# Masked softmax: whole stores held for the load four batches on, and narrow loads as four one-packet transfers

## Chip, cores and metric

One core of a Trainium2 chip runs the whole kernel. The metric is the device time of one execution in microseconds (us); the time of a kernel is the median of its runs.

## What is computed

The reference is a softmax over the last axis of `x`, of shape 16 batches x 8 heads x 256 x 256 in float32. In batch `b` only the first `lengths[b]` columns take part; the others are zero in the result.

```python
for b in range(batch):
    length = lengths[b]
    masked = x[b, :, :, :length].copy()
    masked = masked - np.max(masked, axis=-1, keepdims=True)
    exp_masked = np.exp(masked)
    result[b, :, :, :length] = exp_masked / np.sum(exp_masked, axis=-1, keepdims=True)
```

The lengths of this input are, for batches 0 to 15: 188, 233, 229, 243, 195, 252, 165, 210, 222, 180, 209, 157, 159, 199, 214, 248.

## The kernel before

**Tiling.** A batch has 2048 rows of 256 numbers. They lie on 128 partitions with 16 rows each, so a batch is 16 KB per partition and 2 MB in all. The tile `xt` has 8 slots of one batch each; batch `b` lives in slot `b % 8`, and every step works in place.

**Loads.** Batches 0 to 3 are loaded whole by the SP queue (L107 to L111, batch 0 in two halves). Batches 4 to 15 are loaded by the POOL queue (L153 to L160). There the length is read into a register, and a ladder of branches (`pick`, L126) chooses the narrowest of the widths 160, 168, ... 240 that covers it, or the full 256. A narrow load moves only `w` columns of every row, that is rows of 4·w bytes: widths 200, full, 168, 216, 224, 184, 216, 160, 160, 200, 216, full for batches 4 to 15. Ten of the twelve are narrow. A load on POOL is one transfer. Load `n` waits for load `n - 2` (semaphore `s_sw`, L158) and for the store of batch `n - 8`, which frees its slot (`s_st`, L159). The first of them waits for batch 2 (L152).

**Work on a batch.** DVE masks the batch (L195; `clip` writes a very negative number over the columns past the length). ACT takes the exponential of each of the 16 row groups and sums it (L252), in two halves of eight. DVE then divides each half (L219 the reciprocal, L222 the product over 2048 elements). DVE runs one fixed order, L230 ff.: for batch 0 and from batch 4 on it is divide first half of `b`, mask `b + 1`, divide second half of `b`; for batches 1 to 3 the mask comes first.

**Stores.** The SP queue stores each batch in pieces (`parts`, L50): batch 0 whole, 1 to 7 as a half and two quarters, 8 to 12 and 15 as two halves, 13 and 14 whole. A piece waits for the half that it needs (L117), and the first piece of batch `b` for the whole store of batch `b - 2` (L119).

SP, POOL and ACT each have a queue of their own; all transfers run on the same 16 DMA engines.

Of the kernel before, what the change touches and what calls it, by code (L numbers as in the profile page):

```python
# [16 lines left out]
POOL = mybir.EngineType.Pool  # L17
# [3 lines left out]
def kernel(  # L21
# [6 lines left out]
    nc = tc.nc  # L28
    P = nc.NUM_PARTITIONS

    batch, heads, seq_q, seq_k = x.shape
    rows = heads * seq_q
    assert rows % P == 0
    nt = rows // P
    half = nt // 2
    quarter = nt // 4

    x_f = x.rearrange("b h q k -> b (h q) k").rearrange("b (p t) k -> b p t k", p=P)
    out_f = out.rearrange("b h q k -> b (h q) k").rearrange("b (p t) k -> b p t k", p=P)

    slots = 8
    ahead = 4
    assert slots - ahead == 4 and batch % slots == 0

    widths = list(range(160, 248, 8))
# [1 line left out]
    mid = seq_k // 2  # L47
    big = 1.0e30

    def parts(b):  # L50


        if b == 0:
            cuts = [0, nt]
        elif b < 8:
            cuts = [0, half, half + quarter, nt]
        elif b < 13 or b == batch - 1:
            cuts = [0, half, nt]
        else:
            cuts = [0, nt]  # L60
        return [slice(i, j) for i, j in zip(cuts, cuts[1:])]

    pool = ctx.enter_context(tc.tile_pool(name="all", bufs=1))
    psum = ctx.enter_context(tc.tile_pool(name="psum", bufs=1, space=bass.MemoryType.PSUM))
    xt = pool.tile([P, slots, nt, seq_k], F32, name="xt")
# [11 lines left out]
    seed = pool.tile([1, 2], F32, name="seed")  # L77

    sem = lambda n: ctx.enter_context(nc.semaphore(n))
    s_st = [sem("s_st0"), sem("s_st1")]  # L80
    with tc.tile_critical(no_gpsimd_drain=True):  # L81
# [3 lines left out]
        s_lenf = sem("s_lenf")  # L85
        s_ld = [sem(f"s_ld{k}") for k in range(ahead + 1)]

        s_sw = [sem("s_sw0"), sem("s_sw1")]

        s_iota = sem("s_iota")  # L90
        s_fill = sem("s_fill")
# [2 lines left out]
        s_exp = sem("s_exp")  # L94
        s_out = sem("s_out")

        def length(engine, at):

            return nc.values_load(  # L99
                at,  # L100
                engines=[engine],
                skip_runtime_bounds_check_because="compared with constants, never an address",
            )
# [3 lines left out]
        for h in range(2):  # L107
            s = slice(h * half, (h + 1) * half)
# [1 line left out]
        for b in range(1, ahead):  # L110
            nc.sync.dma_start(out=xt[:, b], in_=x_f[b]).then_inc(s_ld[b + 1], 16)  # L111

        nc.sync.wait_ge(s_exp, 3)
        for b in range(batch):
            s_b = s_st[b % 2]
            for s in parts(b):
                nc.sync.wait_ge(s_out, 2 * b + (s.stop - 1) // half + 1)  # L117
                if b >= 2 and s.start == 0:
                    nc.sync.wait_ge(s_b, 64 * (b // 2 + 1))  # L119
                nc.sync.dma_start(  # L120
                    out=out_f[b, :, s, :], in_=xt[:, b % slots, s, :]
                ).then_inc(s_b, 16 * ((s.stop - s.start) // quarter))

        def pick(v, n, slot, par, ws):  # L126

            if len(ws) == 1:
                w = ws[0]
                nc.gpsimd.dma_start(  # L130
                    out=xt[:, slot, :, :w], in_=x_n[:, n, :, :w]
                ).then_inc(s_sw[par], 16)
                return
            m = (len(ws) - 1) // 2
            with nc.gpsimd.If(v <= ws[m]):  # L135
                pick(v, n, slot, par, ws[: m + 1])
            with nc.gpsimd.Else():
                pick(v, n, slot, par, ws[m + 1 :])

        x_n = x_f.rearrange("b p t c -> p b t c")  # L140
        nc.gpsimd.iota(  # L141
# [1 line left out]
        ).then_inc(s_iota, 1)  # L143
        nc.gpsimd.memset(ones, 1.0).then_inc(s_ones, 1)  # L144
        for par in range(2):
            nc.gpsimd.memset(seed[:, par : par + 1], 0.0).then_inc(s_st[par], 64)  # L146
        nc.gpsimd.wait_ge(s_v, 2)
        for b in range(ahead, slots):
            nc.gpsimd.memset(xt[:, b, :, low:], 0.0).then_inc(s_fill, 1)  # L149
        nc.gpsimd.wait_ge(s_word, 16)  # L150
        nc.gpsimd.wait_ge(s_fill, slots - ahead)
        nc.gpsimd.wait_ge(s_ld[ahead - 1], 16)  # L152
        with nc.Fori(0, (batch - ahead) // 2, 1, engines=[POOL]) as q:  # L153
            for par in range(2):
                n = 2 * q + (ahead + par)
                v_len = length(POOL, word[0:1, bass.ds(2 * n, 1)])
                with nc.gpsimd.If(q >= 1):
                    nc.gpsimd.wait_ge(s_sw[par], 16 * q)  # L158
                    nc.gpsimd.wait_ge(s_st[par], 64 * q)  # L159
                pick(v_len, bass.ds(n, 1), bass.ds(n % slots, 1), par, widths + [seq_k])  # L160


        nc.tensor.wait_ge(s_ones, 1)
# [4 lines left out]
        v = 0  # L168

        def step(ins):  # L170
# [8 lines left out]
                out=down, in0=iota_i, scalar1=0.5, scalar2=-big, op0=ALU.add, op1=ALU.mult  # L179
# [7 lines left out]
                out=len_s, in0=len_f, scalar1=big, scalar2=None, op0=ALU.mult  # L187
# [4 lines left out]
        def clip(b, s, lo, hi):  # L192

            t = xt[:, b % slots, s, lo:hi]
            return nc.vector.scalar_tensor_tensor(  # L195
                out=t,
                in0=down[:, None, lo:hi].to_broadcast([P, s.stop - s.start, hi - lo]),
                scalar=len_s[:, b : b + 1],
                in1=t,
                op0=ALU.add,  # L200
                op1=ALU.min,
            )

        def mask(b, s):
            v_len = length(DVE, word[0:1, 2 * b : 2 * b + 1])
            if b == 0:
                nc.vector.wait_ge(s_ld[s.start // half], 16)
            elif b < ahead:
                nc.vector.wait_ge(s_ld[b + 1], 16)
            else:  # L210
                nc.vector.wait_ge(s_sw[b % 2], 16 * ((b - ahead) // 2 + 1))
            with nc.vector.If(v_len < mid):  # L212
                clip(b, s, 0, mid)
            clip(b, s, mid, seq_k).then_inc(s_min, (s.stop - s.start) // half)

        def divide(b, h):
# [10 lines left out]
            ).then_inc(s_out, 1)  # L227

        mask(0, slice(0, half))
        mask(0, slice(half, nt))  # L230
        for b in range(batch):


            first = b == 0 or b >= ahead
            if first:
                divide(b, 0)
            if b + 1 < batch:
                mask(b + 1, slice(0, nt))
            if not first:
                divide(b, 0)  # L240
            divide(b, 1)
# [5 lines left out]
        with nc.Fori(0, 2 * batch, 1, engines=[ACT]) as i:  # L247
            nc.scalar.wait_ge(s_min, i + 1)
            at = bass.ds(i % (2 * slots), 1)
            for j in range(half):  # L250
                e = x_h[:, at, j, :]
                ins = nc.scalar.activation(  # L252
                    out=e, in_=e, func=EXP, accum_out=sum_h[:, bass.ds(i, 1), j]
# [3 lines left out]

    with tc.tile_critical(no_gpsimd_drain=True):
        for par in range(2):
            nc.sync.wait_ge(s_st[par], 64 * (batch // 2 + 1))  # L260


# [28 lines left out]
```

## Time and profile before

| | |
|---|---|
| median of 2 runs | 155.91 us (155.79 to 156.03) |
| the profiled execution's span, first to last instruction | 154.7 us, so 1.2 us less than the median |
| DVE busy | 115.7 us, 84 instructions |
| ACT busy | 105.2 us, 514 instructions |
| POOL busy | 19.0 us |
| HBM read, written | 28.51 MB, 33.55 MB |

The trace also holds every DMA packet with its queue, size and duration. q1 is the queue of SP, q0 that of POOL. By size, packets of 4 bytes (the completions) left out:

| queue | packet | count | median ns |
|---|---|---|---|
| q1 | 4096 B (a quarter store, one partition) | 1792 | 162 |
| q1 | 8192 B (a half) | 2688 | 313 |
| q1 | 16384 B (whole) | 768 | 611 |
| q0 | 16384 B (a full-width load) | 256 | 611 |
| q0 | 4320 B (five rows of 864 B) | 1200 | 171 |
| q0 | 4480 B (seven of 640 B, five of 896 B) | 976 | 179 |
| q0 | 4800 B (six rows of 800 B) | 672 | 191 |

So a plain transfer makes one packet of each contiguous run, and a narrow load makes packets of as many rows as pass 4096 bytes. One DMA engine serves 8 of the 128 partitions, which is 128 rows of a batch.

How to read it: a group's busy time says how long the engine worked, not that anything waited for it. "idle before" with a releaser says what ended a wait. The DMA share is the mean over the 16 engines and can pass 1 where packets overlap at their ends.

### The profile page before, as it was taken

The page shows a single profiled execution, that of the slowest core. Times are in us where ns is not written, and L with a number is a line of the kernel's source. Part 1 is how long each engine was busy: PE and PEld are TensorE (multiplying, and loading weights), DVE is VectorE, ACT ScalarE, POOL GpSimd, SP SyncE. Part 2 cuts the span into 40 slices and gives each one's busy share as a digit, 9 for nine tenths or more (in the row PEclk, how much of TensorE's full clock was granted, in tenths as well). Part 3 has the DMA queues.
Part 4 walks back from the last instruction along what each step waited for, and adds up shares of the span by engine and source line. Part 5 has one row for each costly group of instructions (what it writes and reads, how often), then busy time and mean ns, then how long its engine had stood idle before and what let it go on. Part 6 is the DMA issues. An engine that isn't in the chain of part 4 may idle for free.

```text
span 154.7 us, 1324 instructions
## 1 busy us (share of the span) xinstructions
PE 0.2 (0%) x1; PEld 0.1 (0%) x1; DVE 115.7 (75%) x84; ACT 105.2 (68%) x514; POOL 19.0 (12%) x25
## 2 busy tenths in 40 slices
PE   0000000000000000000000000000000000000000
PEld 0000000000000000000000000000000000000000
DVE  1249999952999696979979696969689629796700
ACT  3087799992692959778695959595976906959200
POOL 4910031000220110201111020202001000000000
DMA  4999999999999999999999999999999999999992
GB/s 116 426 449 424 428 398 406 398 407 447 400 410 395 402 409 414 415 417 411 404 424 407 417 408 409 415 416 416 416 417 419 419 448 415 426 445 419 430 421 85
DMA packets 9988, 62.08 MB, mean 401 GB/s; under 512 B 850, under 2 KB 946, under 8 KB 6274
## 3 DMA queue, kind: packets, MB, share of 16 engines
q1 hardware_dynamic: 5904, 41.95, 65.8%
q0 software_dynamic: 4080, 20.12, 32.1%
q14 instruction: 2, 0.02, 0.0%
q10 hardware_dynamic: 2, 0.00, 0.0%
HBM read 28.51 MB, written 33.55 MB: 401 GB/s over the span
## 4 chain that ended last, share of the span: by engine, by line
DMA 55%; DVE 19%; ACT 8%; issue 8%; ACTq 2%; SPq 1%; POOLq 1%; DVEq 0%
DMA xt<-in_x_dram 34%; DMA out_dram<-xt 21%; DVE xt L222 9%; DVE xt L195 9%; ACT xt L252 8%; ACTq L252 2%; DVE inv_sum L219 1%; SPq L109 1%; POOLq L99 0%; SPq L111 0%; SPq L120 0%; DVEq L212 0%; POOLq L135 0%; POOLq L130 0%; ACTq L247 0%
## 5 line engine op out<-in xcount | busy, mean ns | idle before, releaser
L252 ACT ACTIVATE xt<-xt x256 | 102.4, 401 | 37.2 <-DVE xt L195 37.2
L222 DVE TENSOR_TENSOR xt<-xt,inv_sum 128x2048 f32<-128x2048 f32 x32 | 73.4, 2292 | 1.1
L252 ACT ACTIVATION_READ_ACCUMULATOR xt<-xt x256 | 47.9, 187 | 0.0
L195 DVE SCALAR_TENSOR_TENSOR xt<-down,len_s,xt 128x2048 f32<-128x2048 f32 (+1 forms) x17 | 37.8, 2222 | 13.1 <-DMA xt<-in_x_dram 13.0
L130 POOL DMA_DIRECT2D xt<-in_x_dram x12 | 12.8, 1064 | 95.5 <-issue 50.6
L219 DVE RECIPROCAL inv_sum<-row_sum 128x8 f32<-128x8 f32 x32 | 6.3, 198 | 14.4 <-ACT xt L252 14.4
L149 POOL MEMSET xt<- 128x1536 f32 x4 | 5.3, 1386 | 1.1 <-DVE len_s L186 1.1
L244 ACT ACT_TABLE_LOAD x1 | 1.3, 1283 | 1.6 <-SPq L81 1.6
L178 DVE TENSOR_SCALAR down<-iota_i 128x256 f32<-128x256 int32 x1 | 0.3, 297 | 1.6 <-POOL iota_i L141 1.6
L183 DVE CAST len_b<-word 1x16 bf16<-1x16 int32 x1 | 0.2, 163 | 0.4 <-DMA word<-in_lengths_dram 0.4
L186 DVE TENSOR_SCALAR len_s<-len_f 128x16 f32<-128x16 f32 x1 | 0.2, 174 | 0.3 <-PE len_f L165 0.3
L141 POOL IOTA iota_i<- 128x256 int32 x1 | 0.3, 331 | 0.6 <-SPq L81 0.6
L146 POOL MEMSET seed<- 1x1 f32 x2 | 0.3, 162 | 0.0
L244 ACT ACTIVATE warm<-const-float32-0.0 128x1 f32<-128x1 f32 x1 | 0.2, 203 | 0.0
L144 POOL MEMSET ones<- 1x128 bf16 x1 | 0.2, 194 | 0.0
L165 PE MATMUL len_f<-len_b,ones 1*128 1x16 bf16 x1 | 0.2, 164 | 2.6 <-DVE len_b L183 2.6
L275 POOL MEMSET const-float32-0.0<- 128x1 f32 x1 | 0.1, 98 | 0.3 <-issue 0.3
L165 PEld LDWEIGHTS len_f<-len_b,ones 1*128 1x128 bf16 x1 | 0.1, 99 | 2.6 <-POOL ones L144 2.6
L275 POOL MEMSET const-float32-1.0<- 128x1 f32 x1 | 0.1, 98 | 0.0
L275 POOL MEMSET const-bfloat16-1.0<- 128x1 bf16 x1 | 0.1, 98 | 0.0
L275 POOL MEMSET const-uint8-127<- 128x1 uint8 x1 | 0.1, 98 | 0.0
L275 POOL BASE_LOAD x1 | 0.0, 17 | 0.1
## 6 DMA issues: line engine op xcount, KB each, us to landing
out_dram<-xt SPq DMA_DIRECT2D x19, 1024.0 KB
out_dram<-xt SPq DMA_DIRECT2D x14, 512.0 KB
xt<-in_x_dram SPq DMA_DIRECT2D x3, 2048.0 KB, 16.1
out_dram<-xt SPq DMA_DIRECT2D x3, 2048.0 KB
xt<-in_x_dram POOLq DMA_DIRECT2D x3, 1728.0 KB, 16.9
xt<-in_x_dram POOLq DMA_DIRECT2D x2, 2048.0 KB, 18.5
xt<-in_x_dram POOLq DMA_DIRECT2D x2, 1600.0 KB, 16.8
xt<-in_x_dram POOLq DMA_DIRECT2D x2, 1280.0 KB, 14.8
```

The source lines that it names most:

```text
L109: nc.sync.dma_start(out=xt[:, 0, s], in_=x_f[0, :, s]).then_inc(s_ld[h], 16)
L130: nc.gpsimd.dma_start(out=xt[:, slot, :, :w], in_=x_n[:, n, :, :w]).then_inc(s_sw[par], 16)
L141: nc.gpsimd.iota(iota_i, pattern=[[1, seq_k]], base=0, channel_multiplier=0).then_inc(s_iota, 1)
L146: nc.gpsimd.memset(seed[:, par : par + 1], 0.0).then_inc(s_st[par], 64)
L149: nc.gpsimd.memset(xt[:, b, :, low:], 0.0).then_inc(s_fill, 1)
L165: nc.tensor.matmul(len_f, lhsT=ones, rhs=len_b, start=True, stop=True).then_inc(s_lenf, 1)
L195: return nc.vector.scalar_tensor_tensor(out=t, in0=down[:, None, lo:hi].to_broadcast([P, s.stop - s.start, hi - lo]), scalar=len_s[:, b : ...
L219: step(nc.vector.reciprocal(out=inv_sum[:, b, s], in_=row_sum[:, b, s]))
L222: nc.vector.tensor_tensor(out=t, in0=t, in1=inv_sum[:, b, s, None].to_broadcast([P, half, seq_k]), op=ALU.mult,).then_inc(s_out, 1)
L244: nc.scalar.activation(out=warm, in_=nc.const_aps.tensor(0.0, (P, 1), F32), func=EXP)
L252: ins = nc.scalar.activation(out=e, in_=e, func=EXP, accum_out=sum_h[:, bass.ds(i, 1), j])
L275: nc = _bacc.Bacc("TRN2", target_bir_lowering=False, num_devices=1)
```

## The change

The stores lose their pieces: each batch is one transfer of 2 MB. Store `b` now waits, besides both of its halves and store `b - 2`, until load `b + 4` has landed. POOL keeps four loads in flight in place of two, each with a semaphore of its own (`s_sw[0]` to `s_sw[3]`); load `n` waits for load `n - 4` and for store `n - 8`. The first POOL load waits for batch 1 in place of batch 2, and that wait stands behind the reading of the length. A narrow load is issued as four transfers, each of four rows of every partition, with `single_packet=True`; a full-width load stays one transfer. The wait for ACT ahead of the first store (L113) goes. The loop on POOL runs three times over four loads in place of six times over two. The order of work on DVE and ACT is the same.

```diff
-    def parts(b):
-        ...
+    lead = 4
+    pieces = 4
+    waves = (batch - ahead) // lead
...
-        s_sw = [sem("s_sw0"), sem("s_sw1")]
+        s_sw = [sem(f"s_sw{k}") for k in range(lead)]
...
-        nc.sync.wait_ge(s_exp, 3)
         for b in range(batch):
             s_b = s_st[b % 2]
-            for s in parts(b):
-                nc.sync.wait_ge(s_out, 2 * b + (s.stop - 1) // half + 1)
-                if b >= 2 and s.start == 0:
-                    nc.sync.wait_ge(s_b, 64 * (b // 2 + 1))
-                nc.sync.dma_start(
-                    out=out_f[b, :, s, :], in_=xt[:, b % slots, s, :]
-                ).then_inc(s_b, 16 * ((s.stop - s.start) // quarter))
+            nc.sync.wait_ge(s_out, 2 * b + 2)
+            if b + lead < batch:
+                nc.sync.wait_ge(s_sw[b % lead], 16 * pieces * (b // lead + 1))
+            if b >= 2:
+                nc.sync.wait_ge(s_b, 16 * (b // 2 + 1))
+            nc.sync.dma_start(out=out_f[b], in_=xt[:, b % slots]).then_inc(s_b, 16)
...
             if len(ws) == 1:
                 w = ws[0]
-                nc.gpsimd.dma_start(
-                    out=xt[:, slot, :, :w], in_=x_n[:, n, :, :w]
-                ).then_inc(s_sw[par], 16)
+                if w == seq_k:
+                    nc.gpsimd.dma_start(
+                        out=xt[:, slot, :, :w], in_=x_n[:, n, :, :w]
+                    ).then_inc(s_sw[k], 16 * pieces)
+                    return
+                for i in range(pieces):
+                    r = slice(i * nt // pieces, (i + 1) * nt // pieces)
+                    nc.gpsimd.dma_start(
+                        out=xt[:, slot, r, :w], in_=x_n[:, n, r, :w], single_packet=True
+                    ).then_inc(s_sw[k], 16)
                 return
...
-        nc.gpsimd.wait_ge(s_ld[ahead - 1], 16)
-        with nc.Fori(0, (batch - ahead) // 2, 1, engines=[POOL]) as q:
-            for par in range(2):
-                n = 2 * q + (ahead + par)
+        with nc.Fori(0, waves, 1, engines=[POOL]) as q:
+            for k in range(lead):
+                n = lead * q + (ahead + k)
                 v_len = length(POOL, word[0:1, bass.ds(2 * n, 1)])
+                if k == 0:
+                    with nc.gpsimd.If(q < 1):
+                        nc.gpsimd.wait_ge(s_ld[2], 16)
                 with nc.gpsimd.If(q >= 1):
-                    nc.gpsimd.wait_ge(s_sw[par], 16 * q)
-                    nc.gpsimd.wait_ge(s_st[par], 64 * q)
+                    nc.gpsimd.wait_ge(s_sw[k], 16 * pieces * q)
+                    nc.gpsimd.wait_ge(s_st[k % 2], 32 * q + 16 * (k // 2))
```

`mask` on DVE waits for the load's own semaphore in the same way, and the last lines of the kernel wait for 16 per store in place of 64.

More of the change, by code (lines that the diff above doesn't have):

```diff
@@ L35 @@
     half = nt // 2
-    quarter = nt // 4
     x_f = x.rearrange("b h q k -> b (h q) k").rearrange("b (p t) k -> b p t k", p=P)
@@ L48 @@
     big = 1.0e30
-    def parts(b):
[L53 to L61, printed above, removed]
+    lead = 4
+    pieces = 4
+    waves = (batch - ahead) // lead
+    assert waves * lead == batch - ahead
     pool = ctx.enter_context(tc.tile_pool(name="all", bufs=1))
@@ L111, with pick @@
             nc.sync.dma_start(out=xt[:, b], in_=x_f[b]).then_inc(s_ld[b + 1], 16)
-        nc.sync.wait_ge(s_exp, 3)
         for b in range(batch):
             s_b = s_st[b % 2]
-            for s in parts(b):
-                nc.sync.wait_ge(s_out, 2 * b + (s.stop - 1) // half + 1)
-                if b >= 2 and s.start == 0:
-                    nc.sync.wait_ge(s_b, 64 * (b // 2 + 1))
-                nc.sync.dma_start(
-                    out=out_f[b, :, s, :], in_=xt[:, b % slots, s, :]
-                ).then_inc(s_b, 16 * ((s.stop - s.start) // quarter))
-        def pick(v, n, slot, par, ws):
+            nc.sync.wait_ge(s_out, 2 * b + 2)
[4 more added lines that the diff above has]
+            nc.sync.dma_start(out=out_f[b], in_=xt[:, b % slots]).then_inc(s_b, 16)
+        def pick(v, n, slot, k, ws):
             if len(ws) == 1:
                 w = ws[0]
-                nc.gpsimd.dma_start(
-                    out=xt[:, slot, :, :w], in_=x_n[:, n, :, :w]
-                ).then_inc(s_sw[par], 16)
+                if w == seq_k:
[8 more added lines that the diff above has]
+                    ).then_inc(s_sw[k], 16)
                 return
@@ L135, in pick @@
             with nc.gpsimd.If(v <= ws[m]):
-                pick(v, n, slot, par, ws[: m + 1])
+                pick(v, n, slot, k, ws[: m + 1])
             with nc.gpsimd.Else():
-                pick(v, n, slot, par, ws[m + 1 :])
+                pick(v, n, slot, k, ws[m + 1 :])
         x_n = x_f.rearrange("b p t c -> p b t c")
@@ L145 @@
         for par in range(2):
-            nc.gpsimd.memset(seed[:, par : par + 1], 0.0).then_inc(s_st[par], 64)
+            nc.gpsimd.memset(seed[:, par : par + 1], 0.0).then_inc(s_st[par], 16)
         nc.gpsimd.wait_ge(s_v, 2)
@@ L151 @@
         nc.gpsimd.wait_ge(s_fill, slots - ahead)
-        nc.gpsimd.wait_ge(s_ld[ahead - 1], 16)
-        with nc.Fori(0, (batch - ahead) // 2, 1, engines=[POOL]) as q:
-            for par in range(2):
-                n = 2 * q + (ahead + par)
+        with nc.Fori(0, waves, 1, engines=[POOL]) as q:
+            for k in range(lead):
+                n = lead * q + (ahead + k)
                 v_len = length(POOL, word[0:1, bass.ds(2 * n, 1)])
+                if k == 0:
+                    with nc.gpsimd.If(q < 1):
+                        nc.gpsimd.wait_ge(s_ld[2], 16)
                 with nc.gpsimd.If(q >= 1):
-                    nc.gpsimd.wait_ge(s_sw[par], 16 * q)
-                    nc.gpsimd.wait_ge(s_st[par], 64 * q)
-                pick(v_len, bass.ds(n, 1), bass.ds(n % slots, 1), par, widths + [seq_k])
+                    nc.gpsimd.wait_ge(s_sw[k], 16 * pieces * q)
+                    nc.gpsimd.wait_ge(s_st[k % 2], 32 * q + 16 * (k // 2))
+                pick(v_len, bass.ds(n, 1), bass.ds(n % slots, 1), k, widths + [seq_k])
         nc.tensor.wait_ge(s_ones, 1)
@@ L210, in mask @@
             else:
-                nc.vector.wait_ge(s_sw[b % 2], 16 * ((b - ahead) // 2 + 1))
+                k = b - ahead
+                nc.vector.wait_ge(s_sw[k % lead], 16 * pieces * (k // lead + 1))
             with nc.vector.If(v_len < mid):
@@ L259 @@
         for par in range(2):
-            nc.sync.wait_ge(s_st[par], 64 * (batch // 2 + 1))
+            nc.sync.wait_ge(s_st[par], 16 * (batch // 2 + 1))
 _INS = ['x', 'lengths']
```

## The prediction

> **What bounds the kernel now.** I read the page's DMA rows first, because DVE (75% busy) and ACT (68%) leave room that the DMA engines do not.
>
> ```profile
> DMA  4999999999999999999999999999999999999992
> GB/s 116 426 449 424 428 398 406 398 407 447 400 410 395 402 409 414 415 417 411 404 424 407 417 408 409 415 416 416 416 417 419 419 448 415 426 445 419 430 421 85
> DMA packets 9988, 62.08 MB, mean 401 GB/s; under 512 B 850, under 2 KB 946, under 8 KB 6274
> q1 hardware_dynamic: 5904, 41.95, 65.8%
> q0 software_dynamic: 4080, 20.12, 32.1%
> ```
>
> The DMA row is full from the second slice to the last but one, so 62.08 MB at some 415 GB/s is a floor as long as the rate stays. The rate itself is not constant. The stage view has it (columns: stretch, length, busy time of PE, PEld, DVE, ACT, POOL, clock, DMA share, GB/s):
>
> ```profile
> 8.00:12.00 4.00, 0.00 (x0) 0.00 (x0) 1.77 (x3) 3.85 (x19) 0.38 (x1) 1.00 0.99 426
> 104.00:110.00 6.00, 0.00 (x0) 0.00 (x0) 5.97 (x4) 4.12 (x22) 1.15 (x1) 1.00 1.02 416
> 134.00:138.00 4.00, 0.00 (x0) 0.00 (x0) 3.97 (x4) 2.12 (x12) 0.00 (x0) 1.00 1.06 449
> 138.00:142.00 4.00, 0.00 (x0) 0.00 (x0) 2.82 (x3) 4.00 (x22) 0.00 (x0) 1.00 1.00 426
> ```
>
> Whole loads alone (8 to 12) and stores of 8 and 16 KB alone (134 to 142) run at 426 to 449, narrow loads beside stores in pieces at 416. Next, the timeline of DVE, the mask rows of batches 3, 4, 12, 13, 14 and 15:
>
> ```profile
> 25.98 2.34 DVE L195 SCALAR_TENSOR_TENSOR xt<-down,len_s,xt 128x2048 f32<-128x2048 f32 x1
> 37.62 2.35 DVE L195 SCALAR_TENSOR_TENSOR xt<-down,len_s,xt 128x2048 f32<-128x2048 f32 x1 [4.42 <-DMA xt<-in_x_dram]
> ...
> 105.84 2.34 DVE L195 SCALAR_TENSOR_TENSOR xt<-down,len_s,xt 128x2048 f32<-128x2048 f32 x1
> 114.83 2.35 DVE L195 SCALAR_TENSOR_TENSOR xt<-down,len_s,xt 128x2048 f32<-128x2048 f32 x1 [0.52 <-DMA xt<-in_x_dram]
> 126.58 2.35 DVE L195 SCALAR_TENSOR_TENSOR xt<-down,len_s,xt 128x2048 f32<-128x2048 f32 x1 [3.29 <-DMA xt<-in_x_dram]
> 134.97 2.34 DVE L195 SCALAR_TENSOR_TENSOR xt<-down,len_s,xt 128x2048 f32<-128x2048 f32 x1
> ```
>
> Between 47.21 and 97.46 the masks come six steps apart, so every 8.38 us, with no wait for a load: divide (2.45), mask (2.38), ACT's half (3.53) form a loop of their own. This loop is nearly as long as the DMA's time for a batch (62.08 MB / 16 at 416 GB/s: 9.3 us). So there are two bounds close together, the DMA work and this chain, and both have to be summed. The chain waits for DMA three times: at batch 4 (mask 3's batch was divided by 33.2, mask 4 starts at 37.62), at batch 13 (114.83 − 105.84 − 8.38 = 0.61) and at batch 14 (126.58 − 114.83 − 8.38 = 3.38). Last, POOL's own rows:
>
> ```profile
> 20.85 1.29 POOL L130 DMA_DIRECT2D xt<-in_x_dram  x1 [12.46 <-issue]
> 38.75 1.16 POOL L130 DMA_DIRECT2D xt<-in_x_dram  x1 [14.15 <-issue]
> ```
>
> The load issued at 38.75 moved its first packet at 43.56, though the load before it had no data packet left from 42.26 on: 4.8 us to make a narrow load of 2048 rows ready.
>
> **The DMA work, part by part.** Per engine, from the packet records. From 8192 to 16384 bytes a packet grows by 298 ns, so 27.5 bytes a ns, and 14 ns are left over for each packet. Five rows of 864 bytes by this are 157 + 14 = 171 ns, as recorded: a further row in a packet costs nothing that shows. *Stores*: 112 packets of 4 KB, 152 of 8 KB, 24 of 16 KB take 18.1 + 47.6 + 14.7 = 80.4 us; 128 of 16 KB take 78.2. Saved 2.2. *Narrow loads*: q0's 32.1% of 154.7 is 49.7 us; less the two full loads (16 packets of 616 ns mean, 9.9) is 39.8. After, 15.93 MB / 16 engines / 27.5 is 36.2, plus 40 packets of 14 ns, 36.8. Saved 3.0. Completions: 53 transfers become 64, eleven of 9 ns, nothing. In sum 5.2 us. The last completion lay at 153.04 and the span's end 1.66 behind it, so DMA alone would end the span at 153.04 − 5.2 + 1.66 = 149.5, if the engines stay as full. They should: with four loads and two stores allowed at a time, either queue has work when the other waits.
>
> A 26 KB packet is longer than any in this trace. Its extra cost is bounded by 0 and by what packing saves (3.0 us); I take 0, since time grows in a straight line from 4 to 16 KB.
>
> The Trainium skill speaks against the packing: "DMA: Bandwidth & Descriptors", section "Why small descriptors are slow (HBM only)", holds that joining descriptors is worth it only up to 256 bytes each, and these rows have 640 to 896. By that rule the 3.0 us would not come; it is the first rival.
>
> **The chain.** *Load 4 comes earlier.* Before, batch 2 landed at 18.6 and load 4 was issued at 20.85. Batch 1 landed at 13.7, so the issue moves to about 15.9, and a piece of 512 rows is ready between 1.2 us (a quarter of 4.8) and 4.8 us later; I take 2.6, near the quarter since work by rows is the simplest reading, so 18.5. *Load 3 comes later.* It is queued on SP since 3.3 us and has eight packets of 611 ns per engine from 17.3 on. The two queues share the engines packet by packet (28 to 36 us: q0 41 to 56%). Two packets go before 18.5; beside the other six, four pieces of load 4 (800-byte rows: 25.6 KB, 945 ns each) and two packets of load 5 take their turns: 3.78 + 1.22 = 5.0 us. Load 3 lands at 28.9 in place of 23.9, mask 3 starts at 29.1 in place of 25.98, 3.1 late, and mask 4 at 33.2 + 3.1 = 36.3, 1.3 us before 37.62. Ends: 0 and 6.2 us of delay, so 33.2 to 39.4.
>
> *Later loads.* Slots free up as before with store n − 8, but loads get larger turns, 26 KB to a store packet's 16, where they had 4.4 KB to 4 or 8. So a load is through within some 10 us of its issue, batches 13 and 14 are in before their masks, and 0.61 + 3.38 = 4.0 us of waits go. The held stores cost nothing here: store b waits for load b + 4, which on this count is issued when store b − 4 is done, three stores earlier. If this cover fails, the stores stop while loads alone run, which the share of q0 would show.
>
> *POOL.* 40 pieces and two full loads replace twelve transfers. A row of 1.15 us for 2048 rows and 0.56 for a full load's 128 gives about 0.7 per piece, and 0.65 of ladder and registers go ahead of each; 4 × 1.35 = 5.4 us a load, beside stores 9 us apart. Hidden. What is queued behind POOL's waits is only later loads.
>
> *The end.* ACT and DVE finish batch 15 at 146.62 − 1.3 − 4.0 = 141.3. Before, half of that store was already gone; now all 2 MB wait for it. Issue to first packet 1.05 (first load: 1.13 to 2.18), eight packets 4.9, spread of the engines and receipt 1.25 (first load) to 2.3 (last store before), then 1.2 to the span's end: 8.4 to 9.5, I take 9.0, the middle, as neither row has both the drained queue and the direction. The span ends at 150.3, behind the 149.5 of the DMA work. With the 1.2 between span and median: **151.5 us**, 2.8% less. Mask 4's ends give 149.5 (DMA binds) to 153.4, so 150.7 to 154.6.
>
> **Rivals.** *Packing brings nothing*, because the flag leaves packets as they are, or because long ones cost what short ones did. For it: no packet above 16 KB in the trace, and the skill's rule; against: the 14 ns. DMA work then saves 2.2 us, ends the span at 152.5, time 153.7, within 2%.
>
> *The making of transfers on POOL becomes the bound.* Place: between POOL's issue and the first packet. The 4.8 us could be a fixed price of a transfer. Load 15 must be in by 141.3 − 11.65 = 129.6 (mask to end of batch 15 took 11.65), forty pieces from 15.9 on, so it decides from (129.6 − 15.9) / 40 = 2.8 us per piece. At 3.6, between that and 4.8, forty take 144 us, the last lands near 160, and 11.65 + 9.0 + 1.2 follow: 182 us. For it: 4.8 us is the only row; against: POOL's own rows shrink from 1.15 to 0.56 us with fewer descriptors. The built program for POOL also grows from 110 to 468 listed instructions. The Trainium skill ("Runtime: NRT & Kernel Launch", "Instruction fetch mechanics") says that a branch out of the loaded window stalls for a fetch; no row prices it here, and the sums leave it out.
>
> *Load 3 starves* behind all of loads 4 to 7 instead of sharing: 6.88 MB / 16 / 27.5 is 15.6 us, it lands at 39.5, mask 4 moves to 46.9, and 9.3 − 4.0 later than before gives 151.9 + 9.0 + 1.2 = 162.1. The shared stretch from 28 to 36 speaks against it.
>
> **How the numbers follow.** About 2% (3.1 us) is what a measurement of this kernel tells from no change: faster means below 152.8, slower above 159.0. The forecast has 0.62, of which I put 0.56 below 152.8 and 0.06 above; packing for nothing 0.20; POOL 0.12; load 3 starving 0.06. So faster 0.56, same 0.26, slower 0.18. The range runs from 149.0 (mask 4 early and the spread at its least) to 157.5, between the second rival's place and the fourth's, which leaves out POOL's and starving's 0.18.
>
> **What would show it.** Right: q0 packets of 20 to 29 KB at 27 bytes a ns, GB/s near 430 through the middle, masks 8.38 us apart to the end without a wait, and the last store alone behind DVE. Wrong: packets of 4.4 KB on q0; gaps between one piece and the next on q0 with stores idle beside them; a wait of several us at mask 3.

## The result, and the profile after

The changed kernel takes 172.73 us (172.71 to 172.74, 2 runs) where the kernel before takes 155.91: a ratio of 1.106 with a 95% interval of 1.104 to 1.109. It is 16.8 us slower; 151.5 was forecast, with a range from 149.0 to 157.5. The profiled execution has a span of 171.1 us. Of all the runs below, two of the five of b1_pad, its profiled one among them, were in a slower state (186.3 and 187.5 us against 183.0 to 184.6), and its time and ratio leave them out.

The DMA rows of its page, with the row of the instruction queue q14 added:

```profile
DMA  5999984999999999999999898999999596999991
GB/s 134 448 429 433 431 289 186 295 389 411 380 398 384 410 319 359 428 339 397 435 423 364 319 381 245 425 345 364 429 409 395 229 418 291 429 429 429 429 429 73
DMA packets 7878, 62.23 MB, mean 364 GB/s; under 512 B 1010, under 2 KB 1458, under 8 KB 4914
q1 hardware_dynamic: 3024, 41.94, 59.3%
q0 software_dynamic: 4832, 20.12, 33.8%
q14 instruction: 20, 0.16, 0.3%
```

The bytes are the same but for 0.15 MB, and that is q14: 20 packets where the kernel before had 2. The rate is no longer steady. It falls to 186 GB/s at 26 to 30 us (the seventh slice), and there the engines are not even full (a 4 in the DMA row). Stores (q1) went from 5904 packets to 3024, as whole ones should. Loads (q0) went up, from 4080 to 4832, where the prediction had counted, per engine, 40 packets for the ten narrow loads in place of some 230.

Two stages of the early stretch (stretch, length, busy PE, PEld, DVE, ACT, POOL, clock, DMA share, GB/s):

```profile
24.00:28.00 4.00, 0.00 (x0) 0.00 (x0) 3.97 (x4) 4.00 (x22) 0.00 (x0) 1.00 0.86 281
28.00:32.00 4.00, 0.00 (x0) 0.00 (x0) 3.93 (x5) 3.99 (x21) 1.87 (x3) 1.00 0.57 146
```

Of the waits, these rows answer to the reading of before (waiter, what for, us in total, times, longest):

```profile
POOL xt L124 <- issue: 69.1, 11, 11.8
DVE xt L191 <- DMA xt<-in_x_dram: 22.4, 9, 4.6
```

```profile
SPq L110 <- DMA xt<-in_x_dram: 98.2, 10, 16.5
```

SP's stores stand 98.2 us behind loads: that is the hold. DVE waits 22.4 us for loads, where it waited 13.0 in the kernel before. And the loads wait for "issue", which means for nothing that the profile shows. The timeline of POOL has it from the start:

```profile
20.05 3.11 POOL L124 DMA_DIRECT2D xt<-in_x_dram  x4 [11.64 <-issue]
28.86 0.55 POOL L118 DMA_DIRECT2D xt<-in_x_dram  x1 [5.70 <-issue]
30.68 2.97 POOL L124 DMA_DIRECT2D xt<-in_x_dram  x4 [1.27 <-issue]
39.41 2.97 POOL L124 DMA_DIRECT2D xt<-in_x_dram  x4 [5.76 <-issue]
54.20 2.23 POOL L124 DMA_DIRECT2D xt<-in_x_dram  x3 [11.82 <-issue]
```

The first load was due at 15.9 and comes at 20.05, and loads 5 to 7 wait for no semaphore, yet come one after another with gaps of 5.70, 1.27 and 5.76 us. What lies in such a gap shows when POOL's branch and register instructions, which the page does not count as busy, are set beside the packets on q14. Ahead of the first load (start in us, from the trace's records):

```
13.69  POOL  COMPARE_BRANCH  L151   the wait for batch 1 is over
14.53  POOL  COMPARE_BRANCH  L129   last branch of the ladder
14.85  POOL  MOVE            L124
18.13  q14   8192 bytes, 309 ns
20.03  POOL  FUSED_REGOPS    L124
20.05  POOL  DMA_DIRECT2D    L124
```

POOL stands still for 5.2 us in the middle of a row of register instructions, an 8 KB packet arrives on the instruction queue, and 1.9 us after its start POOL goes on. Eleven such gaps of more than 1 us (no semaphore in them) lie between 14 and 102 us, 42.7 us in sum. Ten of them, 2.0 to 6.7 us long, have a packet on q14 inside; the five before 60 us take 4.1 to 6.4 us each. The kernel before has two fetches and no such gap.

So my theory after the result (theory 1): POOL's program (145 instructions as built before, 517 after) no longer fits in what it holds at once, and each pass through the ladder has to fetch code. The rivals: loads and stores take turns badly (theory 2), or the hold empties the engines by itself (theory 3).

### The profile page after: what moved, and what is told of

The parts are those of the page before. It is cut to its first block, busy times and chain, and to the rows that moved or that the text cites. A ratio compares the mean times of both kernels' runs of the same rounds, so it can differ in the third digit from the quotient of the medians.

```text
span 171.1 us, 1388 instructions
## 1 busy us (share of the span) xinstructions
PE 0.2 (0%) x1; PEld 0.1 (0%) x1; DVE 115.9 (68%) x84; ACT 105.3 (62%) x514; POOL 37.2 (22%) x55
## 3 DMA queue, kind: packets, MB, share of 16 engines
q1 hardware_dynamic: 3024, 41.94, 59.3%
q0 software_dynamic: 4832, 20.12, 33.8%
## 4 chain that ended last, share of the span: by engine, by line
DMA 61%; issue 16%; DVE 5%; ACT 4%; POOL 3%; POOLq 2%; ACTq 1%; SPq 1%; DVEq 0%
DMA xt<-in_x_dram 47%; DMA out_dram<-xt 14%; ACT xt L249 4%; DVE xt L191 3%; POOL xt L124 3%; DVE xt L219 2%; POOLq L124 1%; ACTq L249 1%; POOLq L90 1%; SPq L100 0%; POOLq L129 0%; DVE inv_sum L216 0%; POOL xt L118 0%; POOLq L153 0%; POOLq L118 0%
## 5 line engine op out<-in xcount | busy, mean ns | idle before, releaser
L191 DVE SCALAR_TENSOR_TENSOR xt<-down,len_s,xt 128x2048 f32<-128x2048 f32 (+1 forms) x17 | 37.8, 2223 | 22.4 <-DMA xt<-in_x_dram 22.4
L124 POOL DMA_DIRECT2D xt<-in_x_dram x40 | 29.9, 753 | 69.1 <-issue 69.1
L118 POOL DMA_DIRECT2D xt<-in_x_dram x2 | 1.1, 548 | 9.3 <-issue 9.3
```

The source lines that it names most:

```text
L118: nc.gpsimd.dma_start(out=xt[:, slot, :, :w], in_=x_n[:, n, :, :w]).then_inc(s_sw[k], 16 * pieces)
L124: nc.gpsimd.dma_start(out=xt[:, slot, r, :w], in_=x_n[:, n, r, :w], single_packet=True).then_inc(s_sw[k], 16)
L191: return nc.vector.scalar_tensor_tensor(out=t, in0=down[:, None, lo:hi].to_broadcast([P, s.stop - s.start, hi - lo]), scalar=len_s[:, b : ...
```

## The experiments

All ratios are against the kernel before, run on the same chip beside them (its median there 155.9 to 156.2 us), with 95% intervals.

**First round: which part holds the 16.8 us.**

```diff
# a1_straight: the widths of this input written in, no ladder, no loop
-        with nc.Fori(0, waves, 1, engines=[POOL]) as q:
-            ...
+        nc.gpsimd.wait_ge(s_ld[2], 16)
+        for n in range(ahead, batch):
+            q, k = divmod(n - ahead, lead)
+            if q >= 1:
+                nc.gpsimd.wait_ge(s_sw[k], 16 * pieces * q)
+                nc.gpsimd.wait_ge(s_st[k % 2], 32 * q + 16 * (k // 2))
+            pick(None, slice(n, n + 1), slice(n % slots, n % slots + 1), k, [drawn[n]])
# a2_nohold
-            if b + lead < batch:
-                nc.sync.wait_ge(s_sw[b % lead], 16 * pieces * (b // lead + 1))
# a3_nosingle
-                        out=xt[:, slot, r, :w], in_=x_n[:, n, r, :w], single_packet=True
+                        out=xt[:, slot, r, :w], in_=x_n[:, n, r, :w]
# a4_onepiece: as a3, and
-    pieces = 4
+    pieces = 1
```

> The changed kernel with the widths of this input written into the program, so that POOL's ladder of branches and its loop are gone (42 transfers in a row); waits, pieces, flag and held stores are the same. Theory 1 (fetching of POOL's code): the gaps of about 5 us between a branch and POOL's next instruction, each with an 8 KB packet on q14 in it, go; loads are issued as soon as their waits end, and the time falls by 12 to 20 us, to 152 to 160. Theory 2 (narrow loads flagged as one packet crowd out the stores or are read slowly): nothing of that changes, 168 to 173. Theory 3 (held stores leave the DMA engines empty whatever POOL does): 166 to 172.

> The changed kernel without the stores' wait for the load four batches on; all else, the long POOL program too, stays. Theory 1: POOL still stalls, but stores fill the DMA engines meanwhile, so some of the loss comes back: 160 to 168. Theory 2: 168 to 173. Theory 3: the hold is the loss, 152 to 158.

> The changed kernel without the one-packet flag, with the same four transfers for each narrow load and the same length of program. Theory 1: POOL stalls as before, 169 to 175. Theory 2: stores get their turns back, 155 to 162. Theory 3: 169 to 173.

> The changed kernel with a narrow load as one transfer without the flag (POOL's program is about half as long), held stores and four loads in flight stay. Theory 1: fewer or no stalls on q14, 152 to 160. Theory 2: as without the flag, 155 to 162. Theory 3: 166 to 172.

| kernel | us | ratio |
|---|---|---|
| a1_straight | 159.33 | 1.020 (1.018 to 1.022) |
| a2_nohold | 174.96 | 1.119 (1.117 to 1.122) |
| a3_nosingle | 173.04 | 1.109 (1.106 to 1.112) |
| a4_onepiece | 158.66 | 1.016 (1.014 to 1.018) |

Both kernels with a short POOL program win back most of the 16.8 us; both with the long one do not. The page and POOL's timeline of a1:

```profile
q14 instruction: 2, 0.02, 0.0%
```

```profile
14.03 3.11 POOL L124 DMA_DIRECT2D xt<-in_x_dram  x4 [5.80 <-DMA xt<-in_x_dram]
17.13 0.55 POOL L118 DMA_DIRECT2D xt<-in_x_dram  x1
17.67 5.93 POOL L124 DMA_DIRECT2D xt<-in_x_dram  x8
```

The first load goes out at 14.03 and the next three right behind it, with no gap. Theories 2 and 3 both fall as causes of the main loss: they had 166 to 173 for a1. On a2 my own theory missed too. It had some of the time back without the hold; the kernel became slower by another point. So the hold, on balance, costs nothing even while POOL stalls.

**Is it the length of the program?** A ladder that is not walked saves branches and register loads besides code. Three runs separate that: code that is never carried out, added to the kernel before; the ladder taken away from the kernel before; and the changed kernel with ladder and loop, but fewer widths.

```diff
# b1_pad, on the kernel before
                 w = ws[0]
+                if w in (176, 192, 208, 232, 240):
+                    for _ in range(40):
+                        nc.gpsimd.memset(seed, 0.0)
# b2_straight: the kernel before with the widths written in, as a1
# c1_fewer_widths, on the changed kernel
-    widths = list(range(160, 248, 8))
-    low = widths[0]
+    widths = [176, 200, 224]
+    low = 160
```

> The kernel before with 400 instructions added to POOL's program that are never carried out (40 small fills in each of the ladder's branches for the widths 176, 192, 208, 232 and 240, which no batch of this input takes); every transfer, wait and store is as before. Theory 1 (fetching of POOL's code is what the change mainly pays for): 8 KB packets on q14 and gaps of about 5 us between a branch and the next instruction appear, loads come late, 162 to 172. Rival (the fetches hurt only where held stores leave the DMA engines empty): the gaps appear, but stores and the other load fill them, 155 to 159.

> The kernel before with the widths of this input written in, without ladder and loop: the control for the same edit on the changed kernel. Theory 1: POOL of before has no stall to lose, 154 to 156.5. If the ladder itself (branches, register loads) is what the edit saved on the changed kernel, it gains here too: below 153.

> The changed kernel with its ladder, loop, flag, whole and held stores, but with four widths in place of twelve (176, 200, 224, 256), which takes POOL's program from 517 to 197 instructions as built; 0.66 MB more are loaded (80 columns more over the ten narrow batches, 8 KB each). Theory 1 (it is the length of the program that stalls POOL, not ladder, registers or loop): no stalls, the 159.3 of the kernel with written-in widths plus 1.5 us for the bytes, 159.5 to 162.5. If the ladder and the loop themselves cost, 165 to 172.

| kernel | POOL instructions as built | q14 packets | us | ratio |
|---|---|---|---|---|
| before | 145 | 2 | 155.91 | |
| b2_straight | no ladder | 1 | 156.07 | 0.999 (0.998 to 1.001) |
| b1_pad | 545 | 35 | 183.37 | 1.173 (1.171 to 1.176) |
| the changed kernel | 517 | 20 | 172.73 | 1.106 (1.104 to 1.109) |
| c1_fewer_widths | 197 | 3 | 161.72 | 1.036 (1.032 to 1.040) |

b1_pad moves the same packets as before (its page has 5904 and 4080 on q1 and q0) and is 17% slower by instructions that no one carries out. Its loads start with the same kind of gap (the profiled execution has a span of 184.7 us):

```profile
25.57 1.30 POOL L133 DMA_DIRECT2D xt<-in_x_dram  x1 [17.18 <-issue]
36.66 0.56 POOL L133 DMA_DIRECT2D xt<-in_x_dram  x1 [9.79 <-issue]
```

```profile
q14 instruction: 35, 0.29, 0.4%
```

The second load of before left at 24.04; here it leaves at 36.66. In b1's records 24 gaps add up to 112.7 us, and every one has a packet on q14 inside. The direction was as expected, the size was not (162 to 172). One load's share of the code is twice as long here (545 instructions over two loads in the loop, against 517 over four), which would fit the 35 packets against 20. b2 shows that the ladder itself costs nothing here, and c1 came in where length alone put it, with its 0.66 MB more. That the stalls come from fetching POOL's code is shown.

**Second round: the 3.2 us that are left in a1.** Two candidates: whole stores, or the hold.

```diff
# a7_straight_parts: a1 with stores cut as before (parts(b)), held at their first piece
+            for s in parts(b):
+                nc.sync.wait_ge(s_out, 2 * b + (s.stop - 1) // half + 1)
+                if s.start == 0:
+                    if b + lead < batch:
+                        nc.sync.wait_ge(s_sw[b % lead], 16 * pieces * (b // lead + 1))
+                    ...
# a5_straight_nohold: a1 without the hold
```

> The changed kernel with the widths written in, and its stores cut again as before (a half and two quarters for batches 1 to 7, halves for 8 to 12 and 15), held as a whole for the load four batches on. Theory A (16 KB store packets leave a narrow load only a fifth of the engines, so loads run late and then alone, at 314 to 380 GB/s): the share of q0 beside stores goes from about 20% back to 37 to 45%, the stretches with loads alone shrink, 151 to 156. Theory B (the hold itself makes these stretches): 157 to 160, as with whole stores.

> The changed kernel with the widths written in and without the stores' wait for the load four batches on. Theory A: whole stores crowd the loads out even more, DVE waits longer for loads, 160 to 166. Theory B: without the hold no stretch has loads alone, 152 to 157.

a7 takes 157.16 us, ratio 1.007 (1.005 to 1.009); a5 takes 163.75, ratio 1.050 (1.048 to 1.052). Theory B falls with a5: without the hold whole stores cost 4.4 us more. Theory A's mechanism is there, but a7 kept 1.1 us, just outside the 151 to 156 that A gave. Two stages of a1, in which hardly any store runs:

```profile
44.00:48.00 4.00, 0.00 (x0) 0.00 (x0) 3.08 (x3) 3.07 (x15) 1.94 (x3) 1.00 0.96 319
84.00:88.00 4.00, 0.00 (x0) 0.00 (x0) 1.93 (x2) 0.93 (x6) 2.97 (x4) 1.00 1.04 363
```

and the same stretches in a7:

```profile
44.00:48.00 4.00, 0.00 (x0) 0.00 (x0) 3.47 (x3) 2.69 (x13) 0.00 (x0) 1.00 1.03 408
84.00:88.00 4.00, 0.00 (x0) 0.00 (x0) 3.97 (x4) 2.12 (x12) 1.16 (x2) 1.00 1.03 407
```

The engines are full in all four. In a1 the packet records give q0 a fifth of what moves beside a store (72 to 76 us: 74 of 414 GB/s) and nearly all of it between stores; in a7 q0 has 34 to 72% of the engines' time in every 4 us from 40 to 124 us, where its loads end. So a whole store goes through ahead of the load, the next store is held until that load is in, and the load then runs alone, at 319 to 363 GB/s. Per engine, the shares of the two queues in time (share times span) say what each part cost: stores 101.8 us before, 99.5 in a1; loads 49.7 before, 54.5 in a1. Together that is 2.5 us more, most of the 3.2. In a7 it is 101.4 and 50.9.

**The rest, and whether some version is faster.**

```diff
# a9_onepiece_parts: the changed kernel with pieces = 1, no flag, stores cut as before (ladder kept)
# a10_onepiece_parts_nohold: a9 without the hold
# a11_onepiece_halves: a9 with cuts = [0, half, nt] for every batch from 1 on
```

> The changed kernel with a narrow load as one transfer (ladder kept, no flag) and the stores cut again as before; held stores, four loads in flight and the earlier first load stay. Theory: what is left of the loss (157.2 with four transfers) is the early stretch of narrow loads alone, 24 to 32 us, and the 30 transfers more; one transfer each gives 155.5 to 157. If four loads in flight or the hold cost nothing in themselves, it comes out at or below the kernel before, 154 to 156.

> The same without the hold. If the hold only orders work that the DMA engines do anyway, the same within 0.5 us; if it keeps loads ahead of stores as with whole stores (159.3 against 163.8), 1 to 4 us slower; if it makes stretches of narrow loads alone, 1 us faster.

> The changed kernel with a narrow load as one transfer and with every store from batch 1 on in two halves; hold and four loads in flight stay. 8 KB packets against 4.4 KB give loads about 35% of the engines beside stores. Fewer quarter packets save 0.6 us of DMA work against the kernel with the stores cut as before: 154.5 to 156.5. If a share of 35% leaves narrow loads to run alone later, 157 to 158.5.

| kernel | us | ratio |
|---|---|---|
| a9_onepiece_parts | 156.48 | 1.003 (1.001 to 1.004) |
| a10_onepiece_parts_nohold | 157.08 | 1.006 (1.004 to 1.008) |
| a11_onepiece_halves | 157.55 | 1.009 (1.006 to 1.012) |

One transfer in place of four is worth 0.4 points (a7 to a9, which also has the ladder and no flag; b2 and a6 show nothing for either), the hold 0.3 (a10 is 0.6 us slower than a9, between the two forecasts), and quarters instead of halves 0.7 (a11 came in at the upper of its two forecasts). So the smaller packets on the store queue seem worth more than the 0.6 us of packets that they cost. Nothing here beats the kernel before.

**Third round: two terms of the sum.** Does the flag do anything, and why are narrow loads slow alone?

```diff
# a6_straight_nosingle: a1 without single_packet=True
# d1_rows768, on a1: 192 columns for the batches with 168, 184, 160 and 160
-        drawn = [256] * 4 + [200, 256, 168, 216, 224, 184, 216, 160, 160, 200, 216, 256]
+        drawn = [256] * 4 + [192 + 8, 256, 192, 216, 224, 192, 216, 192, 192, 200, 216, 256]
```

> The changed kernel with the widths written in and without the one-packet flag, so that what the flag does is seen with POOL's stalls out of the way. If the flag changes nothing (packets on q0 stay at 4.3 to 4.8 KB, share beside whole stores about 20%): 158.5 to 160 as with it. If it made longer turns for loads after all: more than 1.5 us away from 159.3, either way.

> The changed kernel with the widths written in, and 192 columns (rows of 768 bytes) for the batches that had 168, 184, 160 and 160; 0.79 MB more are loaded. In earlier traces one engine took 28 ns for a row of 640 bytes and 37 to 38 ns for rows of 672, 736, 800, 864 and 896 bytes where narrow loads ran alone. If a row is charged in whole steps of 256 bytes from some point on, 768 bytes take 28 ns (436 GB/s alone) and the time is within 1 us of 159.3 although more is moved. If each row longer than 640 bytes has a price of 37 to 38 ns, these rows do too (327 GB/s alone) and the time rises by 1 to 3 us.

a6 takes 159.56 us, ratio 1.022 (1.020 to 1.024), against 159.33 and 1.020 with the flag: the same. Its packets on q0 are the same too, 4320 to 4800 bytes and a remainder, in the same numbers. d1 (one run) takes 161.26. Where a piece of 512 rows ran alone, the time from its completion to the next, over 32 rows an engine, was 37.5 ns a row for 768 bytes in most pieces, 36 to 38 ns in most for 672 to 896 bytes in the other traces, and 26 to 30 ns in most for 640 bytes. The packets themselves are longer: one of 4800 bytes takes 229 ns alone in a1 (25 to 27.3 us), against 191 in the kernel before. So above 640 bytes the price is by the row, not by the byte; what sets it is open. With whole rows of 1024 bytes next to each other the price is 611 / 16 = 38 ns, so alone, a narrow load of more than 640 bytes a row saves next to nothing over a full one. Beside stores it does: 171 ns for five rows of 864 bytes is 34 ns.

## Why the prediction was wrong

**The step that failed** is the paragraph on POOL: 5.4 us a load, "Hidden", with the fetches named in the second rival and then put aside: "no row prices it here, and the sums leave it out". The growth from 110 to 468 listed instructions stood in the prediction; its price is most of the result. About 13.4 of the 16.8 us are POOL's stalls (172.73 to 159.33 when the code is short). The Trainium skill's rule on branches ("Runtime: NRT & Kernel Launch", "Instruction fetch mechanics") is borne out: in the ten gaps with a fetch POOL stood still for 2.0 to 6.7 us each time, nine times right behind a branch. The second rival had the right engine and the wrong mechanism. It put the price on making transfers ready. The first piece, issued at 20.05, moved data at 22.21, 2.2 us later, and in a1 4.2 us later (14.03 to 18.19), where I had 2.6; behind it two pieces of load 4 in a1 ended 1.2 us after the piece before, far under the 2.8 us a piece at which this rival decides.

**"The held stores cost nothing here."** The reason given was wrong, for the stores stood 98.2 us behind loads, and 90.4 in a1, where POOL does not stall; while a load is late, from 24 to 32 us, neither queue fills the engines. The conclusion held, and more by luck than by the count: without the hold the kernel is slower, with the long program (a2, 174.96 against 172.73) as with the short one (a5, 163.75 against 159.33).

**The DMA work: 2.2 us saved on stores, 3.0 on loads.** The first term was right: 101.8 to 99.5 us in a1, a saving of 2.3. The second had the wrong sign: 49.7 to 54.5, 4.8 us lost. The packets were never joined, as the first rival had it; and a further row "costs nothing that shows" only beside stores. Five rows of 864 bytes took the 171 ns that confirmed the line beside stores; alone they take 192 (a1, 46 to 50 us). The count of 64 transfers is one too many (16 stores, 5 loads on SP, 42 on POOL), which is worth 9 ns.

**"Loads get larger turns, 26 KB to a store packet's 16."** The reverse: 4.4 KB to 16, a fifth. That share is what turns packet by packet give, as assumed. Load 3 hardly moved (landed at 24.8 in a1, forecast 28.9, before 23.9).

**The chain.** Right once POOL does not stall, and worth nothing. In a7 load 4 is in before its mask, the masks from batch 5 to 13 are 8.38 us apart, one wait of 1.68 us is left at batch 14, and the last mask starts at 128.25 where it was 134.97:

```profile
109.73 2.35 DVE L204 SCALAR_TENSOR_TENSOR xt<-down,len_s,xt 128x2048 f32<-128x2048 f32 x1
119.87 2.35 DVE L204 SCALAR_TENSOR_TENSOR xt<-down,len_s,xt 128x2048 f32<-128x2048 f32 x1 [1.68 <-DMA xt<-in_x_dram]
128.25 2.34 DVE L204 SCALAR_TENSOR_TENSOR xt<-down,len_s,xt 128x2048 f32<-128x2048 f32 x1
```

The chain gained 6.7 us and the kernel lost 1.1. In a9 DVE waits for no load from batch 4 on, DVE's last product ends at 138.0 where it was 146.6, and the time is that of the kernel before within 0.4 us. Only the DMA work set the end: "two bounds close together" gave the chain a part in the sum that it did not have.

## What to carry to other kernels

Count the instructions of a loop with branches as a resource: here 145 to 253 as built ran with at most one stall of some 2 us and 517 with ten, and on the engine that issues loads a stall of 4 to 6 us falls on everything behind it; padding that is never carried out finds this out in one run. A price read from packets that share the engines holds for that mix alone: ask what runs beside them after the change. When the DMA row is full, sum the DMA work alone; freeing another chain moves nothing.

## What had not been expected

Branching over code costs even where it is never run (b1_pad: 35 fetches, 17%). A fetch brings 8 KB and POOL goes on some 1.5 to 2 us after its last packet starts, but that packet itself comes 0.3 to 5 us after POOL's last instruction. Rows of 672 to 896 bytes loaded alone mostly take 36 to 38 ns each on an engine, whatever their length, and 640 bytes 26 to 30. The one-packet flag on POOL's transfers left packets, turns and time as they were.
